# One fused decoder step on one Trainium2 core: the store of a finished output tile moves from the sync engine's queue to GpSimd's

## Chip, cores and metric

One core of one Trainium2 chip runs the whole kernel. The metric is the device time of one execution in microseconds (us). The kernel before takes 1848.58 us, the median of three runs.

## What is computed

The reference is one inference step of a hybrid decoder layer with D_MODEL 1024, for a prompt of 2048 tokens and a sample group of 8 sequences with 8 tokens each. Cut to what matters here:

```python
h = rms_norm(x, norm_pre)
proj = einsum('btd,de->bte', h, w_in)          # one projection, split below
oa = differential attention (q, k, v)           # group A
ob = causal conv + RG-LRU                       # group B
oc = rwkv7_mix(...)                             # group C: state S, token by token
od = s5_mix(...)                                # group D
o = concatenate([oa, ob, oc, od]) * silu(gate)
y = x + rms_norm(einsum('bte,ed->btd', o, w_out), norm_post)
```

The change concerns the last line only: `y` is made in 17 tiles, sixteen of 128 tokens by 1024 columns (512 KB) and one of 64 tokens for the sample group.

## The kernel before

The program runs through stages: input norm and projection, attention over the prompt, attention of the samples beside the S5 group, and at the end (from about 1170 us on) the RWKV group for the 16 prompt blocks and the samples together with the output projection. Only that last stage matters here.

An RWKV block of 128 tokens is a step of the last stage. `rw_prep` (L1105) loads its projections (`r_X`, L1114, and `r_xv`, L1117) and makes decays and keys. `rw_mats` (L1182) forms small matrices on TensorE, masks them on VectorE (L1207, L1209, L1211) and reduces their diagonal blocks to the tile `r_de` (L1214). `r_de` is stored to a small DRAM tensor `zd` (L1217) and read back, spread over groups of partitions, as `r_zr` (L1221), both by the sync engine. `rw_base` (L1252) then inverts the diagonal blocks in 15 dependent steps on VectorE, each one product into `r_x16w` (L1262) and one addition (L1263); the first product needs `r_zr`. `rw_tri`, `rw_chain` and `rw_norm` finish the block: the recurrent state `r_Z` goes through TensorE, ScalarE, GpSimd (`r_sd`, L1364) and VectorE (L1372), and the group norm gives `r_yo`.

The output of tile i goes through `out_gate` (L1514), which loads the other groups' outputs `o_o` (L1521) and the gates `o_g` (L1523, one buffer) and `o_g2` (L1525) and multiplies them on VectorE (L1526), through `out_prep` (L1532), which scales and splits the result into the float16 tile `o_h`, and through `out_tile` (L1568). `out_tile` loads the residual into `o_x` (L1573, two buffers), runs 48 matmuls (L1584), lets ScalarE take them out of PSUM into `o_y` and sum their squares (L1588, L1590), has VectorE work out the inverse norm in single-column operations (L1592 to L1594 with the helper at L99 to L111) and scale `o_y` (L1597), and has GpSimd add `o_y` into `o_x` in two halves of 512 columns (L1599; in the last tile VectorE adds the second half). L1600 stores `o_x` to `out_y`.

The order of the work is not written out by hand. The source gives an order of calls, with some matmuls tied to others; from it the framework's list scheduler, run with a timeline of its own (`schedule_with_timeline_sim=True`, L1955), makes one fixed order of instructions for each engine when the program is built. Each engine then works through its row in order, so an instruction that waits holds up all behind it. The sync engine (SP in the views) does nothing but begin transfers in this order; GpSimd is POOL, VectorE is DVE, TensorE is PE and ScalarE is ACT.

Of the kernel before, what the change touches and what calls it, by code (L numbers as in the profile page):

```python
# [53 lines left out]
class Part:  # L54
# [1513 lines left out]
    def out_tile(self, i, h, sc, pool, psum, spine=()):  # L1568

        nc = self.nc  # L1570
        t0, n = P * i, min(P, TT - P * i)
        x = pool.tile([P, D], F32, name="o_x", bufs=OB[2])
        nc.sync.dma_start(x[:n], self.i["x"][t0:t0 + n])  # L1573
        ss = pool.tile([P, 4], F32, name="o_ss", bufs=2)
        ys = []
        for g in range(2):
            sl = slice(512 * g, 512 * g + 512)
            a = psum.tile([P, 512], F32, name="acc", bufs=ACB)
            c = 0
            for k in range(KT):  # L1580
                ins = spine[(KT * g + k) * len(spine) // (2 * KT)] if spine else None
                for e, f in ((0, 0), (0, 1), (1, 0)):
                    with self.tc.issue_after(ins) if ins and e == f else ExitStack():
                        nc.tensor.matmul(a[:n].rearrange("p (c n) -> p c n", c=4), h[:, k, e], self.wo[:, 4 * g:4 * g + 4, k, f, :],  # L1584
                                         start=c == 0, stop=c == 3 * KT - 1)
                    c += 1
            y = pool.tile([P, 512], F32, name="o_y", bufs=OB[3])
            nc.scalar.activation(y[:n], a[:n], AF.Copy, scale=sc[:n, 1:2])  # L1588
            jk = pool.tile([P, 6, P], BF16, name="o_j", bufs=1)
            nc.scalar.activation(jk[:n, :4].rearrange("p a b -> p (a b)"), y[:n], AF.Square, accum_out=ss[:n, g:g + 1])  # L1590
            ys.append(y)
        nc.vector.tensor_tensor(ss[:n, 2:3], ss[:n, 0:1], ss[:n, 1:2], op=ALU.add)  # L1592
        nc.vector.tensor_scalar(ss[:n, 2:3], ss[:n, 2:3], 1.0 / D, 1e-6, op0=ALU.mult, op1=ALU.add)
        self.rsqrt(pool, ss[:n, 3:4], ss[:n, 2:3], n, 1, "oq")  # L1594
        for g, y in enumerate(ys):
            sl = slice(512 * g, 512 * g + 512)
            nc.vector.scalar_tensor_tensor(y[:n], y[:n], ss[:n, 3:4], self.npo[:n, sl], op0=ALU.mult, op1=ALU.mult)  # L1597
            eng = nc.vector if i == 15 and g else nc.gpsimd
            eng.tensor_tensor(x[:n, sl], y[:n], x[:n, sl], op=ALU.add)  # L1599
        nc.sync.dma_start(self.o["y"][t0:t0 + n], x[:n])  # L1600

    def rwkv_sample_consts(self, pool):
        nc = self.nc
# [377 lines left out]
```

## Time and profile before

| what | value |
|---|---|
| three runs | 1840.5, 1848.58, 1851.93 us |
| the profiled execution | 1846.33 us |
| span of its instructions | 1844.5 us |
| TensorE busy | 1497.3 us (81% of the span) |
| VectorE busy | 1448.1 us (79%) |
| ScalarE busy | 902.1 us (49%) |
| GpSimd busy | 811.6 us (44%) |
| granted TensorE clock, mean | 0.881 of full speed |

The span goes from the first instruction to the last; the profiled execution's own time has some two microseconds around it. The busy share of an engine is a mean over all stages and says little on one of them, so that the stage with the stores is read by itself: what each engine was busy with in it, what an engine waited for and for how long, and the order of single instructions on one engine in a stretch. In those rows the time at the front is the start in microseconds from the span's start, the next number the duration, and the bracket at the end the idle time of the engine before the instruction and what ended it. In the table by stretches the number in brackets behind a busy time is the count of instructions, and PEld is TensorE's loading of weights. In the lists of waits the three numbers are microseconds in all, times, and the longest.

### The profile page before, as it was taken

How to read it: one execution, taken by the hardware profiler on the slowest of the kernel's cores; microseconds unless marked ns; L12 is line 12 of the kernel's file. 1: busy time of each engine (PE TensorE's matmuls, PEld its weight loads, DVE VectorE, ACT ScalarE, POOL GpSimd, SP SyncE). 2: the span in 40 equal slices, each digit the busy share in tenths (PEclk: the TensorE clock that was granted, in tenths of full speed). 3: DMA queues.
4: the chain of work that ended last, by engine and by line, in shares of the span. 5: the costliest groups of instructions: out<-in, count | busy, mean ns of one | idle time of the engine just before them, and what ended most of it. 6: DMA issues, size and time to landing. Idle time of an engine off the chain costs nothing.

```text
span 1844.5 us, 33323 instructions
## 1 busy us (share of the span) xinstructions
PE 1497.3 (81%) x10956; PEld 844.9 (46%) x10956; DVE 1448.1 (79%) x4619; ACT 902.1 (49%) x2211; POOL 811.6 (44%) x887
## 2 busy tenths in 40 slices
PE   4889888987789788878894899657688887887887
PEld 2445644444344344434442456446455454554443
DVE  7797639988899899889896754376878887888865
ACT  3455746655556566657772222243344454444333
POOL 3441326736668877443344454261324333333312
PEclk9999998999899899989996999875777887887889
DMA  4422144575445655464447877635223233333221
GB/s 147 128 91 93 28 116 117 125 149 117 111 111 139 152 141 146 106 145 115 86 104 199 274 250 238 205 96 163 73 66 100 81 105 93 92 86 102 66 72 58
DMA packets 300898, 225.33 MB, mean 122 GB/s; under 512 B 192531, under 2 KB 248565, under 8 KB 300213
## 3 DMA queue, kind: packets, MB, share of 16 engines
q1 hardware_dynamic: 288388, 184.85, 37.4%
q10 hardware_dynamic: 8496, 24.76, 4.7%
q0 software_dynamic: 3840, 13.61, 2.6%
q8 instruction: 86, 1.41, 0.3%
q14 instruction: 88, 0.71, 0.1%
HBM read 130.04 MB, written 53.24 MB: 99 GB/s over the span
## 4 chain that ended last, share of the span: by engine, by line
DVE 34%; PE 21%; DMA 15%; issue 8%; POOL 4%; ACT 3%; SPq 1%; ACTq 0%; POOLq 0%; DVEq 0%
PE acc L206 7%; DMA r_zr<-zd 5%; DVE a_mx L365 4%; PE acc L1584 4%; DVE a_e L389 4%; DMA a_wt<-a_w 3%; DVE r_x L1263 2%; DVE r_x16w L1262 2%; DVE a_w L395 2%; DMA zd<-r_de 2%; PE ss L511 2%; DVE r_W L1177 1%; PE pf L530 1%; POOL a_e L388 1%; POOL a_w L395 1%
## 5 line engine op out<-in xcount | busy, mean ns | idle before, releaser
L206 PE MATMUL acc<-hT,w 128*128 128x512 f16 (+1 forms) x3120 | 633.6, 353 | 24.7 <-ACT pst L640 4.3
L206 PEld LDWEIGHTS <-w 128*128 128x128 f16 x3120 | 269.7, 101 | 322.3 <-issue 66.8
L368 ACT ACTIVATE a_e<-s,a_mx,sig 128x512 f32<-128x512 f32 (+3 forms) x320 | 226.9, 715 | 122.6 <-DVE a_mx L366 106.4
L1584 PE MATMUL acc<-wo,o_h 128*128 128x512 f16 (+1 forms) x816 | 225.1, 422 | 1.2 <-ACT o_y L1588 0.6
L365 DVE TENSOR_REDUCE a_mx<-s 128x1 f32<-128x512 f32 (+3 forms) x320 | 186.3, 599 | 23.4 <-PE s L361 18.7
L388 POOL TENSOR_SCALAR a_e<-a_e,a_al 128x512 f32<-128x512 f32 (+3 forms) x160 | 114.6, 731 | 148.6 <-DVE a_al L384 119.4
L389 DVE SCALAR_TENSOR_TENSOR a_e<-a_e,a_al 128x512 f32<-128x512 f32 (+3 forms) x160 | 149.3, 948 | 9.2 <-POOL a_e L388 9.0
L361 PE MATMUL s<-kh,qh 128*128 128x512 f16 (+3 forms) x320 | 105.7, 359 | 38.2 <-ACT a_e L368 35.0
L402 PE MATMUL pv<-vtok,a_wt 128*128 128x128 f16 x544 | 70.0, 230 | 64.6 <-DMA a_wt<-a_w 57.9
L392 ACT CAST a_w<-a_e 128x512 f16<-128x512 f32 (+3 forms) x160 | 86.3, 557 | 69.9 <-DVE a_e L389 63.5
L1584 PEld LDWEIGHTS <-o_h 128*128 128x128 f16 (+1 forms) x816 | 76.6, 105 | 95.1 <-issue 26.3
L395 POOL TENSOR_TENSOR a_w<-a_e,a_w 128x512 f16<-128x512 f32 (+3 forms) x80 | 90.0, 1128 | 64.4 <-ACT a_w L392 62.4
L1262 DVE TENSOR_TENSOR r_x16w<-r_zr,r_x 128x60 f32<-128x60 f32 (+18 forms) x255 | 58.8, 231 | 67.0 <-DMA r_zr<-zd 63.8
L1599 POOL TENSOR_TENSOR o_x<-o_y,o_x 128x512 f32<-128x512 f32 (+1 forms) x33 | 48.4, 1487 | 121.4 <-DVE o_y L1597 84.7
L402 PEld LDWEIGHTS <-a_wt 128*128 128x128 f16 x544 | 52.2, 104 | 91.4 <-DMA a_wt<-a_w 76.1
L395 DVE TENSOR_TENSOR a_w<-a_e,a_w 128x512 f16<-128x512 f32 (+2 forms) x80 | 76.9, 964 | 2.7 <-ACT a_w L392 2.7
L170 POOL TENSOR_TENSOR hT<-hf,hT 128x512 f16<-128x512 f32 (+1 forms) x36 | 36.5, 1022 | 88.3 <-ACT hT L168 88.2
L403 PE MATMUL pv<-vtok,a_wt 128*128 128x64 f16 x544 | 66.1, 202 | 0.0
L1263 DVE TENSOR_TENSOR r_x<-r_x,r_x16w 128x60 f32<-128x60 f32 (+18 forms) x255 | 62.4, 245 | 3.4
L368 ACT ACTIVATION_READ_ACCUMULATOR a_e<-s,a_mx,sig 128x1 f32 x320 | 64.0, 200 | 0.0
L366 DVE TENSOR_SCALAR a_mx<-a_mx,sig 128x1 f32<-128x1 f32 x320 | 59.8, 201 | 0.4
L511 PE MATMUL ss<-kv,qbd 128*32 128x256 f32 x256 | 52.5, 415 | 6.7 <-DMA kv<-in_ckv 6.5
(552 smaller groups left out, 3378.0 us busy)
## 6 DMA issues: line engine op xcount, KB each, us to landing
kv<-in_ckv SPq DMA_DIRECT2D x128, 256.0 KB
w<-in_w_in ACTq DMA_DIRECT2D x20, 512.0 KB
pc<-pst SPq DMA_DIRECT2D x40, 256.0 KB
xw<-in_xT SPq DMA_DIRECT2D x16, 512.0 KB
w<-in_w_out ACTq DMA_DIRECT2D x16, 512.0 KB
sg<-pst SPq DMA_DIRECT2D x32, 256.0 KB
r_X<-pc SPq DMA_DIRECT2D x16, 512.0 KB
r_zr<-zd SPq DMA_DIRECT2D x16, 512.0 KB
```

The costliest lines, as they stand in the source:

```text
L206: self.nc.tensor.matmul(acc[:, :n], w16[:, k, a, :], h[:, k, e, :], start=(c == 0), stop=(c == 3 * KT - 1))
L361: ins = nc.tensor.matmul(s[:, :kn], q[:, c], kh[:, c, k0:k0 + kn], start=True, stop=True)
L365: nc.vector.tensor_reduce(mx[:, p, c:c + 1], s[:, :kn], axis=AX.X, op=ALU.max, negate=True)
L368: nc.scalar.activation(e[:, :kn], s[:, :kn], AF.Exp, scale=sig, bias=mx[:, p, c:c + 1], accum_out=l[:, p, c:c + 1])
L388: nc.gpsimd.tensor_scalar(e1[:, :kn], e1[:, :kn], al[:, p, 1:2], 0.0, op0=ALU.mult, op1=ALU.add)
L389: nc.vector.scalar_tensor_tensor(e0[:, :kn], e0[:, :kn], al[:, p, 0:1], e1[:, :kn], op0=ALU.mult, op1=ALU.add)
L395: eng.tensor_tensor(w[:, kn:], e0[:, :kn], w[:, :kn], op=ALU.subtract)
L402: ins = nc.tensor.matmul(pv[:, :P], wt[:, j], v, start=kt == 0, stop=kt == qb, skip_group_check=True)
L511: ins = nc.tensor.matmul(sp[g:g + 32, 256 * j:min(256 * j + 256, n)], self.qbd[:, m, s].rearrange("p a q -> p (a q)"), rhs, start=True, st ...
L1262: XV.tensor_tensor(w[:, :, :m], zr[:, k, :, k + 1:], x[:, :, k:k + 1].to_broadcast([P, nu, m]), op=ALU.mult)
L1263: XV.tensor_tensor(x[:, :, k + 1:], x[:, :, k + 1:], w[:, :, :m], op=ALU.add)
L1584: nc.tensor.matmul(a[:n].rearrange("p (c n) -> p c n", c=4), h[:, k, e], self.wo[:, 4 * g:4 * g + 4, k, f, :], start=c == 0, stop=c == 3 * ...
```

## The change

The store of `o_x` to `out_y` is issued by GpSimd in place of the sync engine. Nothing else in the source differs.

```diff
             eng = nc.vector if i == 15 and g else nc.gpsimd
             eng.tensor_tensor(x[:n, sl], y[:n], x[:n, sl], op=ALU.add)
-        nc.sync.dma_start(self.o["y"][t0:t0 + n], x[:n])
+        nc.gpsimd.dma_start(self.o["y"][t0:t0 + n], x[:n])
```

The scheduler makes its orders anew from this source, and from the first store on they differ on every engine. On GpSimd, around the addition into the `o_x` of one tile in the middle of the stage, the row before is:

```order
L1599 TENSOR_TENSOR o_x_19963<-o_y_19991,o_x_19963 128x512
L1599 TENSOR_TENSOR o_x_19963<-o_y_20020,o_x_19963 128x512
L1163 TENSOR_SCALAR r_kf_20623<-r_tha_20575,rwv_15083 128x128
L1139 TENSOR_SCALAR r_thw_20576<-r_thw_20576 128x256
L1163 TENSOR_SCALAR r_kf_20623<-r_tha_20575,rwv_15083 128x128
L1165 TENSOR_SCALAR r_kka_20622<-r_tha_20575 128x256
L1167 TENSOR_TENSOR r_kf_20623<-r_kf_20623,r_X_20562 128x256
L1364 TENSOR_TENSOR r_sd_20362<-r_Z_19862,r_Dp_19752 64x128 x2
```

and now it is:

```order
L1599 TENSOR_TENSOR o_x_19963<-o_y_19991,o_x_19963 128x512
L1599 TENSOR_TENSOR o_x_19963<-o_y_20020,o_x_19963 128x512
L1139 TENSOR_SCALAR r_thw_20576<-r_thw_20576 128x256
L1163 TENSOR_SCALAR r_kf_20623<-r_tha_20575,rwv_15083 128x128
L1165 TENSOR_SCALAR r_kka_20622<-r_tha_20575 128x256
L1600 DMA out_y<-o_x_19963 128x1024
L1167 TENSOR_TENSOR r_kf_20623<-r_kf_20623,r_X_20562 128x256
L1364 TENSOR_TENSOR r_sd_20362<-r_Z_19862,r_Dp_19752 64x128 x2
```

The store stands behind L1139, L1163 and L1165 and not directly behind the addition that it needs. Of the first eleven stores eight stand behind L1165 in this way and three behind the first L1163. The sync engine's row at the same tile is, before:

```order
L1221 DMA r_zr_20254<-zd1_15089 128x1x1024
L1117 DMA r_xv_20977<-pc_1197 128x2x64 x2
L1525 DMA o_g2_20951<-sg3_1201 128x2x128
L1600 DMA out_y<-o_x_19963 128x1024
L1573 DMA o_x_20789<-in_x 128x1024
L1521 DMA o_o_21360<-od3_63 128x6x128
L1114 DMA r_X_21388<-pc_1197 128x8x128
```

and now:

```order
L1221 DMA r_zr_20254<-zd1_15089 128x1x1024
L1525 DMA o_g2_20951<-sg3_1201 128x2x128
L1573 DMA o_x_20789<-in_x 128x1024
L1521 DMA o_o_21360<-od3_63 128x6x128
L1114 DMA r_X_21388<-pc_1197 128x8x128
```

The store has gone, while the load of `o_x_20789` into the same buffer, which has to wait for that store to land, stands where it stood. (The two loads of `r_xv` are now ahead of L1221.) On VectorE the rows that lead up to the same step's `r_de` are, before:

```order
L1209 TENSOR_TENSOR r_ET_20232<-ra_20233,rmask_15067 64x256
L110 SCALAR_TENSOR_TENSOR oq1_20026<-oq1_20026,o_ss_19965 128x1
L1207 TENSOR_TENSOR r_W_20221<-ra_20241,rmask_15067 64x512
L1209 TENSOR_TENSOR r_ET_20232<-ra_20241,rmask_15067 64x256
L1211 TENSOR_TENSOR r_dg_20249<-r_NA_20231,bm4_15077 128x256
L111 SCALAR_TENSOR_TENSOR r_nrs_20092<-nq4_20101,r_nrs_20092 128x4
L111 SCALAR_TENSOR_TENSOR o_ss_19965<-oq1_20026,o_ss_19965 128x1
L1214 TENSOR_REDUCE r_de_20251<-r_dg_20249 128x64
```

and now:

```order
L1593 TENSOR_SCALAR o_ss_19965<-o_ss_19965 128x1
L1207 TENSOR_TENSOR r_W_20221<-ra_20241,rmask_15067 64x512
L1209 TENSOR_TENSOR r_ET_20232<-ra_20241,rmask_15067 64x256
L1211 TENSOR_TENSOR r_dg_20249<-r_NA_20231,bm4_15077 128x256
L1421 TENSOR_SCALAR r_nss_20091<-r_nss_20091 128x4
L99 TENSOR_SCALAR o_ss_19965<-o_ss_19965 128x1
L1526 TENSOR_TENSOR o_o_20947<-o_o_20947,o_g_20949 128x768
L1214 TENSOR_REDUCE r_de_20251<-r_dg_20249 128x64
```

The product L1526, whose end frees the buffer of `o_g` for its next load, now stands right ahead of `r_de`, and the single-column rows of the norm (`o_ss`, `oq`) come later. L1526 stands between `r_dg` and `r_de` in four of the eleven steps from the first store on before, and in six now. Between `r_de` and the first product with `r_zr` VectorE has 247 rows over these eleven steps before and 293 now; the 46 more are nearly all small rows of the two norms.

## Rows read from the trace of the kernel before

**Rows 1.** Two stretches: length, busy PE, PEld, DVE, ACT, POOL, clock, DMA share, GB/s.

```profile
1411.50:1752.00 340.50, 284.03 (x2504) 165.16 (x2503) 285.21 (x1108) 146.80 (x412) 123.89 (x170) 0.82 0.32 90
1752.00:1844.50 92.50, 72.98 (x526) 35.42 (x522) 54.67 (x228) 34.84 (x89) 19.24 (x18) 0.91 0.20 65
```

**Rows 2.** Who VectorE waited for, 1411.5 to 1752: us in total, times, longest.

```profile
DVE r_x16w L1262 <- DMA r_zr<-zd: 39.7, 10, 6.6
...
DVE o_o L1526 <- DMA o_o<-od: 1.4, 2, 1.0
```

**Rows 3.** Who the sync engine's queue waited for, 1380 to 1845.

```profile
SPq L1600 <- POOL o_x L1599: 74.5, 11, 12.1
```

**Rows 4.** The sync engine's transfers in order of time, at two tiles.

```profile
1416.86 0.35 SPq L1600 DMA_DIRECT2D out_y<-o_x  x1
1423.93 0.36 SPq L1525 DMA_DIRECT2D o_g<-sg  x1
...
1663.84 0.36 SPq L1525 DMA_DIRECT2D o_g<-sg  x1
1664.29 0.42 SPq L1600 DMA_DIRECT2D out_y<-o_x  x1
1667.34 0.35 SPq L1573 DMA_DIRECT2D o_x<-in_x  x1
1673.73 0.37 SPq L1521 DMA_DIRECT2D o_o<-od  x1
```

**Rows 5.** GpSimd in order of time, at the second of these tiles.

```profile
1656.09 3.12 POOL L1599 TENSOR_TENSOR o_x<-o_y,o_x 128x512 f32<-128x512 f32 x2 [3.81 <-DVE o_y L1597]
...
1664.89 0.41 POOL L1139 TENSOR_SCALAR r_thw<-r_thw 128x256 f32<-128x256 f32 x1 [5.24 <-ACT r_thw L1137]
...
1665.83 0.51 POOL L1165 TENSOR_SCALAR r_kka<-r_tha 128x256 f32<-128x256 f32 x1
```

**Rows 6.** GpSimd's groups by line: stores that it begins elsewhere; us in all, mean ns.

```profile
L275 POOL DMA_DIRECT2D out_v<-vf x4 | 2.3, 564 | 3.2 <-ACT vtok L273 3.2
```

**Rows 7.** Transfers by issue: stores begun by GpSimd, KB each, median us to landing.

```profile
yd<-s5ys POOLq DMA_DIRECT2D x4, 528.0 KB, 5.3
...
od<-lx POOLq DMA_DIRECT2D x2, 256.0 KB, 2.6
```

**Rows 8.** The slowest of these, the loads of s5E (514 KB): us from issue to landing.

```profile
DMA to landing us min/median/max: 4.2/7.7/12.3
```

**Rows 9.** Who waited for GpSimd, 1380 to 1845: first and last of four entries.

```profile
PEld ra L49 <- POOL r_XY L1270: 1.6, 2, 0.8
...
PEld rl L44 <- POOL r_M L1283: 0.2, 1, 0.2
```

**Rows 10.** VectorE in order of time: r_de and the first product with r_zr.

```profile
1514.36 0.58 DVE L1214 TENSOR_REDUCE r_de<-r_dg 128x64 f32<-128x256 f32 x1
1524.00 0.22 DVE L1262 TENSOR_TENSOR r_x16w<-r_zr,r_x 128x60 f32<-128x60 f32 x1 [2.49 <-DMA r_zr<-zd]
1544.77 0.57 DVE L1214 TENSOR_REDUCE r_de<-r_dg 128x64 f32<-128x256 f32 x1
1555.97 0.22 DVE L1262 TENSOR_TENSOR r_x16w<-r_zr,r_x 128x60 f32<-128x60 f32 x1 [6.28 <-DMA r_zr<-zd]
1593.30 0.39 DVE L1262 TENSOR_TENSOR r_x16w<-r_zr,r_x 128x60 f32<-128x60 f32 x1 [2.63 <-DMA r_zr<-zd]
```

**Rows 11.** The sync engine at the second of these steps.

```profile
1544.88 0.36 SPq L1523 DMA_DIRECT2D o_g<-sg  x1
1545.37 0.45 SPq L1217 DMA_DIRECT2D zd<-r_de  x1
```

**Rows 12.** VectorE's groups by line, 1411.5 to 1752: a single-column row of the norm.

```profile
L110 DVE SCALAR_TENSOR_TENSOR oq<-oq,o_ss 128x1 f32<-128x1 f32 x28 | 4.3, 153 | 0.0
```

**Rows 13.** The sync engine's last transfer, from 1838 on.

```profile
1840.11 0.34 SPq L1600 DMA_DIRECT2D out_y<-o_x  x1
```

**Rows 14.** What the sync engine's queue waited for from 1840 on.

```profile
SPq L1955 <- DMA out_y<-o_x: 2.1, 1, 2.1
```

## The prediction

> **What bounds the kernel now.** I read the views in this order: busy time by stretches, VectorE's waits, the sync engine's waits, then single transfers and instructions in order of time. The stores lie in the last stage, so I begin with the stretch of ten steps from 1411.5 to 1752 us [rows 1]. VectorE is busy for 285.2 of its 340.5 us (84%) and TensorE for 284.0; GpSimd is busy for 123.9 (36%). Nobody there is idle for long, but VectorE's 55.3 us of idleness have one main cause: 39.7 us are waits for `r_zr` in front of the first product of the inversion, about 4 us a step [rows 2]. A step is therefore VectorE's work plus that wait, 34.05 us on average (340.5 over ten). The wait starts a fixed journey after `r_de` (store to `zd`, load back): in one step 9.64 us pass from the start of `r_de` to the first product and VectorE stands still for 2.49 of them, in the next 11.20 us pass and it stands still for 6.28 [rows 10]. How long it stands still depends on how many other instructions the schedule has put between `r_de` and that product, and on how long the journey takes.
>
> The sync engine looks worse than it is. It waits 74.5 us in eleven places for GpSimd's addition before it can store [rows 3], and all its later loads stand behind. But what is behind is not ready either. At 1416.86 it has its store out, and the next transfer, the load of `o_g2`, starts only at 1423.93, because it waits for VectorE [rows 4]. At the tile of 1664 the order is the other way round: the sync engine comes to the store late, at 1664.29, since `o_g2` before it waited; GpSimd had ended its addition at 1659.21 [rows 4, 5]. The view shows the wait that ended last before each transfer, not time that the kernel would get back.
>
> **The change, part by part.**
>
> The sync engine loses 17 issues of some 0.35 us and 74.5 us of waiting. What it gets for them is small, since the load of `o_x` into the stored buffer stays in its row, at about the same place, and it now has to wait there until GpSimd's store has landed. The block moves by one instruction, from the store to the reload. In the tile of 1664 the reload goes out at 1667.34 and the next transfer, `o_o`, at 1673.73 [rows 4], released by something else; `o_o` came late for VectorE by only 1.4 us in ten steps [rows 2]. I value this part at 0; the bound on the good side is those 1.4 us.
>
> GpSimd gets 17 issues. The trace has no store of 512 KB begun by it, but four of 128 KB, which occupy it for 0.564 us each [rows 6]: 17 x 0.564 = 9.6 us on an engine that is idle for 216 us in these ten steps. Behind the store stand products for the keys (L1167), the state's decay (L1364) and L1180; other engines waited for GpSimd only four times from 1380 on, 1.6 us at most and 0.2 at least in one entry [rows 9]. Cover is there, so I take +1 us; if it were gone, eleven stores in the steps would cost 11 x 0.564 = +6.2. The lower bound is 0.
>
> In eight of eleven tiles the store also comes later than GpSimd could give it, because the schedule puts it behind L1139, which waits for ScalarE. In the tile of 1664 L1165 ends at 1666.34 [rows 5], 2.05 us after the sync engine's store began. How long it then takes to land is bounded by a store of 256 KB in 2.6 us and one of 528 KB, of more scattered shape, in 5.3 [rows 7]; I take the middle, 4.0, because the size is that of the second and the shape that of the first. Then the reload goes at about 1670.4, still 3.3 us before `o_o`. Cost 0.
>
> Here the Trainium skill has a price of its own, on the page DMA: Bandwidth & Descriptors, section Anatomy of one DMA: a transfer begun by GpSimd takes about 2.0 us plus its bytes at 436 GB/s, an estimate of 3.2 us for 512 KB. The store of 256 KB took the 2.6 that this rule gives, the one of 528 KB took 2.1 us more than it. By the rule the last store, below, would cost 0.8 and not 1.6.
>
> The new order is the largest term, and it comes from the scheduler, not from the store. Between `r_de` and the first product VectorE now has 46 more rows over eleven steps, nearly all single-column rows of 0.153 us [rows 12], so 46 x 0.153 = 7.0 us of work slips into the wait for `r_zr`: -7.0. Against it, in two more steps L1526 stands right before `r_de`, which lets the load of `o_g` out just before the store to `zd`, as at 1544.88 and 1545.37 [rows 11]. That step's journey was 11.20 us against 9.64, so 2 x 1.56 = +3.1. Together -3.9. The bounds are wide, since ten steps could all become like the shortest, or the six with L1526 before `r_de` all like the long one: from first product to first product one step took 31.97 us and the next 37.33 [rows 10]. Ten short ones would give 10 x (34.05 - 31.97) = -20.8; six long ones among ten, each 37.33 - 34.05 = 3.28 over the mean, +19.7. I take the value from the row counts.
>
> At the end, the last store is on the path. The sync engine began it at 1840.11, was busy for 0.34 us and waited 2.1 more for it [rows 13, 14], so 2.4 in all. GpSimd's would take 4.0: +1.6. The bounds are 2.6 and 12.3 us [rows 7, 8], +0.2 to +9.9.
>
> Sum: 0 + 1 - 3.9 + 1.6 = -1.3 us. Against the profiled execution's own 1846.33 (its span of 1844.5 and 1.8 around it) that is 1845.0. The median of the runs is 2.25 us above that execution, so I forecast 1847.3 for a median, the old 1848.58 less 1.3. A measurement of this kernel can tell about 1% from no change, 18 us.
>
> **Rivals.**
>
> The new order is simply better: every step becomes like the one of 31.97 us. Then 1848.6 - 20.8 + 2.6 (GpSimd and the end) = 1830.4. For it speaks that VectorE's waits for `r_zr` of 39.7 us are there to be filled; against it, that the number of steps with the two long products L1597 between `r_de` and the first product is eight of eleven in both orders, so that only small rows were moved.
>
> The new order is worse at `r_de`: all six steps that have L1526 before it become long, and the moved rows do not fill their waits. That is 1848.6 + 19.7 + 2.6 = 1870.9. For it speaks the pair of steps in [rows 10]; against it, that four steps of before have L1526 there and not all are long, and that the step after a long one is shorter. It decides where zd's store is slowed by `o_g`.
>
> The store lands late: the reload then holds up `o_o` and `r_X` in the sync engine's row, and VectorE waits at L1526. The turning point is a landing time of 1673.73 - 0.35 - 1666.34 = 7.0 us. GpSimd's loads of 514 KB took 7.7 in the median and 12.3 at most [rows 8]. At 10 us the delay is 3.0 in each of eight tiles, 24 us, and 7.6 at the end, with +1: 1848.6 + 32.6 = 1881.2. Against it speaks that those loads were eight, issued in groups, while these are single stores a step apart. The Trainium skill has a reason for it, on the page DMA: Bandwidth & Descriptors, section SWDGE vs HWDGE vs iDMA: GpSimd writes the descriptors into SBUF, which VectorE can lock it out of in some of its modes, and a transfer begun by the sync engine is immune. In this trace GpSimd's issues took 0.564 us beside a working VectorE [rows 6], so nothing shows the lock yet.
>
> The change does not do what it says, in that the sync engine stays blocked at the reload, is no rival but the first term of the sum.
>
> **How the numbers follow.** Forecast 0.60, better order 0.14, worse order at `r_de` 0.17, late landing 0.09. The forecast's own range is 1837 to 1859, from the bounds of GpSimd's term, the end, and about half of the order's. Faster by over 1% (below 1830) takes most of the first rival: 0.13. Slower by over 1% (above 1867) takes nearly all of the late landing and half of the worse order, since not all six need be long: 0.18. Within 1%: 0.69. The range to hold the time 8 times in 10 goes from 1830 to 1868; it leaves out most of the late landing and the lower half of the better order.
>
> **What would show it.** Right: the sync engine's waits at L1600 are gone and its waits at L1573 for the store have grown to a similar sum; GpSimd's L1600 rows are near 0.56 us; VectorE's wait for `r_zr` over the same steps falls to about 36 us; the last store takes 4 us. Wrong: `o_o` or `r_X` turns up among VectorE's or TensorE's waits with more than a few microseconds (late landing), the wait for `r_zr` rises above 50 us (worse order), or the steps shorten by 2 us each (better order). GpSimd's stores well above 0.6 us, or other engines that wait for GpSimd for more than 10 us in all, would break the second term.

## The result and the profile after

The changed kernel takes 1858.32 us in the median (18 runs, 1851.71 to 1865.82) against 1849.63 for the one before (18 runs): a ratio of 1.0052 with a 95% interval of 1.0033 to 1.0071, so 9.6 us slower (6.1 to 13.1; the two medians by themselves lie 8.7 apart). The profiled execution took 1853.88 us with a span of 1852.1, 7.6 over the span before. That is within 1% and inside the 1837 to 1859 that were named, a range wide enough for either sign, but on the other side of the -1.3 us that were forecast.

The two stretches of [rows 1], after (columns as there):

```profile
1411.50:1752.00 340.50, 281.13 (x2479) 166.01 (x2481) 283.16 (x1103) 146.14 (x409) 127.99 (x180) 0.82 0.31 90
1752.00:1852.10 100.10, 77.51 (x545) 38.37 (x545) 57.91 (x231) 35.60 (x91) 23.36 (x25) 0.87 0.18 60
```

In the same 340.5 us VectorE got through 1103 rows where it had 1108, and 100.1 us were left to do where there had been 92.5. Who VectorE waited for from 1411.5 to 1752 (us, times, longest), against [rows 2]:

```profile
DVE r_x16w L1262 <- DMA r_zr<-zd: 33.5, 10, 7.2
DVE o_o L1526 <- DMA o_o<-od: 5.8, 2, 4.1
DVE r_W L1207 <- ACT r_NA L1206: 2.3, 2, 1.7
DVE r_ss L1152 <- PE ra L44: 2.2, 2, 1.3
DVE r_kk L1162 <- PE ra L116: 2.2, 1, 2.2
```

The wait for `r_zr` fell by 6.2 us, from 39.7. The wait for `o_o` grew by 4.4, and waits at `r_W` and `r_kk` stand where the list of before had almost none. The sync engine's largest waits from 1380 on, against [rows 3]:

```profile
SPq L1573 <- DMA out_y<-o_x: 59.4, 8, 14.6
SPq L1525 <- DVE r_x16w L1262: 39.8, 4, 14.4
```

L1600 is gone from them, and the reload L1573 waits in its place. GpSimd's stores, and below them their time to landing; [rows 6 to 8] had only other transfers:

```profile
L1600 POOL DMA_DIRECT2D out_y<-o_x x17: 567/605/622, 1386.3 to 1845.4; - x17
...
DMA to landing us min/median/max: 2.9/2.9/4.9
```

The tile that [rows 4, 5] show at 1664 us, on GpSimd and then on the sync engine:

```profile
1657.79 3.20 POOL L1599 TENSOR_TENSOR o_x<-o_y,o_x 128x512 f32<-128x512 f32 x2 [0.75 <-DVE o_y L1597]
...
1662.00 0.41 POOL L1165 TENSOR_SCALAR r_kka<-r_tha 128x256 f32<-128x256 f32 x1
1662.35 0.60 POOL L1600 DMA_DIRECT2D out_y<-o_x  x1
```

```profile
1668.71 0.41 SPq L1573 DMA_DIRECT2D o_x<-in_x  x1
1675.91 0.36 SPq L1521 DMA_DIRECT2D o_o<-od  x1
```

The store begins 1.36 us after its addition ended, and lands some 3 us later, still before the reload at 1668.71; `o_o` follows 7 us behind that.

For the rest I cut both traces at the same rows: from the first product with `r_zr` of one step to that of the step eleven later, from there to the start of VectorE's last L1562 (the last `o_h`), and from there to the end. Before, then after:

```profile
1385.70:1761.40 375.70, 312.40 (x2776) 181.09 (x2776) 313.85 (x1225) 162.01 (x452) 132.41 (x184) 0.83 0.31 90
1761.40:1821.30 59.90, 55.82 (x399) 27.39 (x399) 41.24 (x180) 25.98 (x67) 14.61 (x15) 0.91 0.18 60
1821.30:1844.50 23.20, 11.22 (x51) 4.70 (x49) 9.70 (x32) 4.22 (x9) 4.63 (x4) 0.85 0.25 79
```

```profile
1384.70:1763.30 378.60, 315.35 (x2795) 184.63 (x2796) 315.01 (x1238) 163.76 (x455) 137.80 (x195) 0.83 0.31 89
1763.30:1826.10 62.80, 55.96 (x380) 28.05 (x379) 42.19 (x167) 25.28 (x65) 16.44 (x18) 0.88 0.17 58
1826.10:1852.10 26.00, 11.24 (x51) 4.72 (x49) 9.75 (x32) 4.24 (x9) 6.51 (x7) 0.82 0.21 71
```

So 2.9 us more in the steps, 2.9 behind the last step with 19 matmuls fewer, and 2.8 at the end, less 1.0 that this execution was ahead at the start. The first two can be the new order or the stores; the experiments take the two apart.

### The profile page after: what moved, and what is told of

Read it like the earlier page. It is cut to its first block, busy times and chain, and to the rows that moved or that the text cites. A ratio compares the mean times of both kernels' runs of the same rounds, so it can differ in the third digit from the quotient of the medians.

```text
span 1852.1 us, 33295 instructions
## 1 busy us (share of the span) xinstructions
PE 1495.8 (81%) x10956; PEld 846.9 (46%) x10956; DVE 1451.7 (78%) x4619; ACT 904.2 (49%) x2211; POOL 822.0 (44%) x904
## 4 chain that ended last, share of the span: by engine, by line
DVE 32%; PE 22%; DMA 15%; issue 8%; POOL 5%; ACT 4%; SPq 1%; ACTq 0%; POOLq 0%; DVEq 0%
PE acc L206 6%; PE acc L1584 5%; DMA r_zr<-zd 5%; DVE a_mx L365 4%; DVE a_e L389 3%; DMA a_wt<-a_w 3%; DVE a_w L395 2%; DVE r_x16w L1262 2%; DMA zd<-r_de 2%; PE ss L511 1%; DVE r_x L1263 1%; POOL a_e L388 1%; PE rc L44 1%; PE pf L530 1%; DVE r_W L1177 1%
## 5 line engine op out<-in xcount | busy, mean ns | idle before, releaser
L395 POOL TENSOR_TENSOR a_w<-a_e,a_w 128x512 f16<-128x512 f32 (+3 forms) x80 | 89.7, 1124 | 59.4 <-ACT a_w L392 57.3
L1262 DVE TENSOR_TENSOR r_x16w<-r_zr,r_x 128x60 f32<-128x60 f32 (+18 forms) x255 | 66.5, 261 | 61.5 <-DMA r_zr<-zd 58.5
L1599 POOL TENSOR_TENSOR o_x<-o_y,o_x 128x512 f32<-128x512 f32 (+1 forms) x33 | 49.1, 1502 | 117.7 <-DVE o_y L1597 90.7
L1263 DVE TENSOR_TENSOR r_x<-r_x,r_x16w 128x60 f32<-128x60 f32 (+18 forms) x255 | 59.8, 235 | 3.2
L1364 POOL TENSOR_TENSOR r_sd<-r_Z,r_Dp 64x128 f32<-64x128 f32 x64 | 29.6, 463 | 72.3 <-DVE r_Z L1372 65.6
L366 DVE TENSOR_SCALAR a_mx<-a_mx,sig 128x1 f32<-128x1 f32 x320 | 60.2, 203 | 0.4
```

What stands on the lines that cost most here:

```text
L395: eng.tensor_tensor(w[:, kn:], e0[:, :kn], w[:, :kn], op=ALU.subtract)
L1262: XV.tensor_tensor(w[:, :, :m], zr[:, k, :, k + 1:], x[:, :, k:k + 1].to_broadcast([P, nu, m]), op=ALU.mult)
L1263: XV.tensor_tensor(x[:, :, k + 1:], x[:, :, k + 1:], w[:, :, :m], op=ALU.add)
```

## The experiments

**How the order is held.** Both programs trace the same instructions under the same numbers; only the engine of 17 of them differs. So a kernel can be given any wanted row: a table lists, for each engine from just before the first store on, the numbers in order, and each is tied behind the one ahead of it, without a wait.

```diff
         program(tc, ins, outs)
+        pin(tc)
...
+def pin(tc):
+    rows = {i.name: i for i in tc.nc.cur_bb.bb.instructions}
+    dep = mybir.DependencyInfo(mybir.DependencyClass.NoSync, mybir.DependencyReason.DATA)
+    for row in ROWS.split(";"):
+        n, last = 0, None
+        for d in row.split():
+            n += int(d)
+            i = rows[f"I-{n}"]
+            if last:
+                tc.add_manual_dep(i, last, dep, reason="row")
+            last = i.name
```

The old order is that of before, the new one that of after. The table itself costs nothing that can be seen: old_sync_quarters, which is before with its stores in quarters, has a ratio of 1.0003, and new_pool_direct, which is after with its stores a few rows earlier, 1.0050 where after has 1.0052. All runs in one table; the times in us are from one trace each, cut as above, "last step" being the eleventh step and "close" the time from the end of VectorE's last L1599 to the end of the span (good to some 0.05 us, since spans are read in tenths). The ratio is that of times to the kernel before, with its interval.

| run | order, stores | 11 steps | last step | behind it | close | ratio |
|---|---|---|---|---|---|---|
| before | old, sync | 375.7 | 29.3 | 59.8 | 4.45 | |
| after | new, GpSimd | 378.7 | 33.2 | 62.8 | 7.22 | 1.0052 (1.0033 to 1.0071) |
| old_order_pool | old, GpSimd | 376.0 | 30.4 | 59.5 | 7.24 | 1.0033 (1.0004 to 1.0061) |
| new_order_sp | new, sync | 376.2 | 33.4 | 62.9 | 4.46 | 1.0030 (1.0003 to 1.0056) |
| old_order_last_pool | old, last GpSimd | 373.4 | 30.3 | 57.9 | 6.34 | 1.0026 (1.0001 to 1.0052) |
| new_order_last_sp | new, last sync | 381.3 | 33.8 | 61.6 | 5.52 | 1.0080 (1.0047 to 1.0113) |
| new_last_sp_again | the same | 379.4 | 33.8 | 62.0 | 5.49 | 1.0044 (1.0022 to 1.0067) |
| new_then_old | mixed, sync | 373.2 | 30.3 | 57.9 | 4.14 | 1.0011 (0.9989 to 1.0033) |
| old_then_new | mixed, sync | 377.4 | 32.0 | 61.4 | 4.44 | 1.0028 (1.0002 to 1.0053) |
| new_yc_early | new, sync | 376.6 | 34.2 | 60.2 | 4.45 | 1.0004 (0.9983 to 1.0024) |
| after_yc_early | new, GpSimd | 375.1 | 33.6 | 60.2 | 7.25 | 1.0053 (1.0034 to 1.0073) |
| new_pool_direct | new, GpSimd | 379.6 | 33.6 | 62.6 | 7.30 | 1.0050 (1.0028 to 1.0071) |
| new_og_late | new, sync | 374.7 | 34.5 | 61.9 | 4.14 | 1.0045 (1.0023 to 1.0067) |
| old_fill | old, sync | 366.4 | 31.2 | 58.1 | 4.22 | 0.9962 (0.9940 to 0.9984) |
| old_fill2 | old, sync | 368.5 | 30.5 | 55.3 | 4.17 | 0.9941 (0.9918 to 0.9964) |
| old_pool_but_last | old, last sync | 370.6 | 30.2 | 59.3 | 5.51 | 1.0006 (0.9987 to 1.0025) |
| old_pool_quarters | old, last sync | 378.9 | 30.9 | 60.3 | 9.17 | 1.0040 (1.0022 to 1.0058) |
| old_sync_quarters | old, sync | 375.3 | 30.7 | 60.2 | 4.19 | 1.0003 (0.9986 to 1.0019) |

An interval is some 4 us to either side, so a term of 3 us is not read from one run's time. The columns of single stretches repeat far better: the last step took 29.3 to 30.9 us in the six traces with nothing but the old order and 33.2 to 33.8 in the five with nothing but the new one, the stretch behind it 57.9 to 60.3 and 61.6 to 62.9.

**Order and store apart.** old_order_pool:

```diff
  L1599 TENSOR_TENSOR o_x<-o_y,o_x 128x512 x2
+ L1600 DMA out_y<-o_x
  L1163 TENSOR_SCALAR r_kf<-r_tha,rwv 128x128
```

> The order of every engine is held as in the kernel before, by a table of instruction numbers; only the 17 stores move, each from the sync engine's row to GpSimd's, directly behind the addition that it needs. The changed kernel was 9.6 us over the one before. Theory O (the new order costs it, the store itself only at the end of the program): 2.5 to 3 us over before, all of it behind the last addition. Theory S (the store on GpSimd's row and its later landing cost it): 7 to 10 us over before, with o_o among VectorE's waits as in the changed kernel (5.8 us) and GpSimd's later rows awaited. Theory Q (neither, a change of the whole program such as code or semaphores): under 1 us.

new_order_sp (the same source lines as before; on the sync engine's row):

```diff
  L1525 DMA o_g2<-sg3
+ L1600 DMA out_y<-o_x
  L1573 DMA o_x<-in_x
```

> The order of every engine is held as in the changed kernel; only the 17 stores move back to the sync engine's row, ahead of the load into the same buffer, as they stood before. Theory O: 6 to 7 us over before (the 9.6 less the end's 2.8), with steps of the last stage 0.3 us longer on average than in before and the same stretch behind the last step longer by 2 to 3 us. Theory S: within 2 us of before. Under O, VectorE's waits for r_zr over the steps stay near the changed kernel's 41.6 us; under S the longer steps go.

Each of the two alone costs something: 6.1 us for the store in the old order (0.7 to 11.3) and 5.5 for the order (0.6 to 10.3). In the traces the store adds nothing to the steps of the old order and 2.8 us to the close; the order adds to the last step and the stretch behind, with the stores back on the sync engine and the waits for `o_o` unchanged at 5.7 us. In old_order_pool they are 1.0 us over the same steps. So that wait belongs to the order. By the times alone neither theory can be ruled out, since both intervals reach into what theory S expected; it is the columns and these waits that speak for theory O.

**The end.** old_order_last_pool and new_order_last_sp:

```diff
-        nc.sync.dma_start(self.o["y"][t0:t0 + n], x[:n])
+        (nc.gpsimd if i == 15 else nc.sync).dma_start(self.o["y"][t0:t0 + n], x[:n])
```

```diff
-        nc.gpsimd.dma_start(self.o["y"][t0:t0 + n], x[:n])
+        (nc.sync if i == 15 else nc.gpsimd).dma_start(self.o["y"][t0:t0 + n], x[:n])
```

> Order held as in the kernel before, and only the store of the last tile goes to GpSimd's row, at its end. Theory E (the last store is the whole cost of the store's engine): 2.5 to 3 us over before, the time from the end of VectorE's last addition to the end of the span growing from 4.5 to about 7.2 us. If the landing of a store begun by GpSimd is not slower and only its issue is (0.59 against 0.34): under 1 us.

> Order held as in the changed kernel with its stores on GpSimd, but the store of the last tile goes back to the sync engine. Theory O with E: 2.5 to 3 us under the changed kernel, so 6 to 7 over before. If E is wrong and the end is not what the last store makes it: as the changed kernel, 9 to 10 over before. Theory S allows either, and differs from O by the run with the new order and all stores on the sync engine, which would then be 4 us or more below this one.

Theory E in its simple form falls. The close is 6.34 us with the last store alone on GpSimd, not 7.2, and 5.52 with all but the last there, not 4.45: the sixteen stores that had landed long before add to it as well. The time of new_order_last_sp was above that of the changed kernel and not 3 us under it; the repeat gave 8.1 us over before, so the pair lies around 11 with intervals that overlap. The 8.1 (4.1 to 12.4) lies between what theories A and B expected of the repeat and does not tell them apart.

**Where the order costs.** new_then_old follows the new order up to the first product of the last but one prompt step and then the old, old_then_new the other way round.

> All stores on the sync engine. The rows follow the new order up to the first product of the last but one prompt step and the old order from there. Over three traces of each order the ten steps up to there differ by -6.9 to +6.3 us each and by +0.3 in sum; the last step is 3.5 us longer in the new order and the stretch behind it 3.3. Theory T (the loss of the new order sits in the last step and the stretch behind it): within 1.5 us of before. Theory D (the loss is spread, the prefix leaves work undone that the rest must do): 3 us or more over before, with the last step and the stretch behind it longer than the old order's 30.0 and 59.1 us.

> All stores on the sync engine. The rows follow the old order up to the same place and the new order from there. Theory T: 6 to 7 us over before, the last step near 33.5 us and the stretch from its first product to the last o_h near 62.4. Theory D: 0 to 3 us over before.

Theory T holds by the columns: with ten steps of the new order and the old rest the last step and the stretch behind it are as short as in the old order (30.3 and 57.9), and the time is 1.0011; with the old steps and the new rest the stretch behind is long (61.4) and the time is 1.0028, 5.2 us over before (0.4 to 9.8). Its last step took 32.0, half way and not the 33.5 expected, and both intervals of the time also hold what theory D expected. Single steps differ far more than their sum: the fifth took 38.4 us in the new order and 32.1 in the old, the sixth 30.4 and 37.3 (means of three traces).

In the last step the front of `r_de` is later because more stands ahead of it. From the first product to the end of `r_de`, before and after:

```profile
1732.10:1752.60 20.50, 17.99 (x159) 10.79 (x161) 18.98 (x75) 7.01 (x16) 6.79 (x10) 0.84 0.23 62
```

```profile
1730.10:1754.00 23.90, 22.06 (x204) 13.01 (x204) 21.13 (x78) 9.63 (x27) 7.21 (x12) 0.78 0.25 77
```

The stretch is 3.4 us longer and holds 45 matmuls more, with 4.1 us more of TensorE's time: it is busy for 22.06 of 23.90. That these 45 are the cause is read from the rows, and was not tried by itself. For the stretch behind, VectorE, GpSimd and TensorE in the changed kernel:

```profile
1763.34 0.22 DVE L1262 TENSOR_TENSOR r_x16w<-r_zr,r_x 128x60 f32<-128x60 f32 x1 [5.29 <-DMA r_zr<-zd]
1763.48 0.16 DVE L110 SCALAR_TENSOR_TENSOR nq<-nq,r_nss 128x4 f32<-128x4 f32 x1
1763.55 1.41 DVE L1597 SCALAR_TENSOR_TENSOR o_y<-o_y,o_ss,npo 128x512 f32<-128x512 f32 x2
...
1765.01 1.25 DVE L111 SCALAR_TENSOR_TENSOR r_nrs<-nq,r_nrs 128x4 f32<-128x4 f32 x1
...
1766.31 1.48 DVE L1423 TENSOR_TENSOR r_yc<-r_yc,r_nrs 128x256 f32<-128x256 f32 x1
```

```profile
1764.38 3.13 POOL L1599 TENSOR_TENSOR o_x<-o_y,o_x 128x512 f32<-128x512 f32 x2 [11.97 <-DVE o_y L1597]
```

```profile
1767.93 0.66 PE L49 MATMUL rl<-ident,r_yc 128*128 128x128 f32 x2 [3.05 <-DVE r_x L1263]
...
1770.60 5.36 PE L1584 MATMUL acc<-wo,o_h 128*128 128x512 f16 x15
```

and TensorE before:

```profile
1763.98 0.66 PE L49 MATMUL rl<-ident,r_yc 128*128 128x128 f32 x2 [5.05 <-DVE o_ss L111]
...
1771.11 3.40 PE L1584 MATMUL acc<-wo,o_h 128*128 128x512 f16 x15
```

TensorE needs `r_yc` for L49. Before it has it 2.6 us after the first product (1763.98, the cut at 1761.40), in the changed kernel 4.6, because the two long products L1597 and what they push back stand ahead of L1423. L1597 also lets GpSimd's addition L1599 begin, and beside it L111 takes 1.25 us and L1423 1.48 (elsewhere the same two rows take 0.18 and 0.41, as at 1385.91 and 1386.34 before); the rows do not say why. VectorE stood still for 5.29 us just before, with the two rows and L1423 nearly ready. And 15 matmuls of the same form then take 5.36 us and not 3.40: the granted clock from 1770.6 to 1776.0 was 0.63 in the mean, and from 1767.9 to 1771.0 it was 0.50, which is the lower of the two levels (1.2 GHz); ahead of that, to 1767.9, TensorE had done nothing for 3.0 us. Before, the idleness was longer (5.05 us) but lay earlier, and for these 15 the clock was back (1.00 from 1771.1 to 1774.6). new_yc_early and after_yc_early move three rows:

```diff
+ L110 SCALAR_TENSOR_TENSOR nq<-nq,r_nss 128x4
+ L111 SCALAR_TENSOR_TENSOR r_nrs<-nq,r_nrs 128x4
+ L1423 TENSOR_TENSOR r_yc<-r_yc,r_nrs 128x256
  L1262 TENSOR_TENSOR r_x16w<-r_zr,r_x 128x60
- L110 SCALAR_TENSOR_TENSOR nq<-nq,r_nss 128x4
  L1597 SCALAR_TENSOR_TENSOR o_y<-o_y,o_ss,npo 128x512 x2
  L1263 TENSOR_TENSOR r_x<-r_x,r_x16w 128x60
- L111 SCALAR_TENSOR_TENSOR r_nrs<-nq,r_nrs 128x4
  L1262 TENSOR_TENSOR r_x16w<-r_zr,r_x 128x56
- L1423 TENSOR_TENSOR r_yc<-r_yc,r_nrs 128x256
```

> New order, stores on the sync engine, and only in the last prompt step three rows of VectorE (L110 and L111 of the group norm, and L1423, which makes r_yc) go from behind the first product of the inversion and two products L1597 to directly ahead of it, into the wait for r_zr. Theory M (the stretch behind the last step is longer because TensorE stands still for r_yc and then works at the lower clock): the stretch falls from 62.4 us to 59 or 60, TensorE's wait of 3.2 us for VectorE at L49 goes, and the time is 2 to 3 us over before in place of 5. Theory N (it is longer for other rows of the new order): the stretch stays at 61.5 to 63 us.

> The changed kernel with the same three rows moved, stores on GpSimd. Theory M: 6 to 7 us over before in place of 9.6, the stretch behind the last step 59 to 60 us. Theory N: 9 to 10 over before, the stretch 61.5 to 63.

TensorE in new_yc_early, whose first product stands at 1759.11:

```profile
1759.48 0.63 PE L49 MATMUL rl<-ident,r_yc 128*128 128x128 f32 x2
1763.57 0.48 PE L44 MATMUL rc<-r_Z,r_W 128*64 128x64 f32 x2 [3.45 <-DVE r_Z L1372]
...
1765.64 4.02 PE L1584 MATMUL acc<-wo,o_h 128*128 128x512 f16 x15
```

Theory M holds for the stretch, 60.2 us in both kernels in place of 62.4. Not all as expected: L49 now follows at once, but the idleness moves to the next link, the state `r_Z`: beside L1599 it is now rows of the inversion ahead of it that take 1.28 us (L1263) and 1.18 (L1262). From the first product to the end of the 15 matmuls it is 10.6 us in place of 12.6; 0.7 of the 2.1 come from the earlier start of the 15 and 1.3 from their shorter time (5.36 against 4.02). The time shows it with the stores on the sync engine (1.0004 in place of 1.0030) and not with them on GpSimd (1.0053, 9.8 us over before), where theory N's 9 to 10 us came.

**What moving rows on VectorE is worth.** new_og_late moves one row in eight places. In six of them it stood directly ahead of `r_de`, as below; in the other two it stood six and nine rows ahead:

```diff
- L1526 TENSOR_TENSOR o_o<-o_o,o_g 128x768
  L1214 TENSOR_REDUCE r_de<-r_dg 128x64
+ L1526 TENSOR_TENSOR o_o<-o_o,o_g 128x768
```

> New order, stores on the sync engine, and one row moved on VectorE: where L1526 stands just ahead of r_de (eight places, six of them in the measured steps) it goes directly behind it, so that r_de no longer waits for L1526 and for the load of o_o in front of it. Theory W (VectorE's row is the path: what leaves the front of r_de and falls into the wait for r_zr is gained): the o_o waits of 5.7 us and six times 0.96 us go, 11 us together, so 4 to 5 us under before. Theory G (what is gained at one wait comes back at another): o_o's waits go from the list, but the time falls by 4 us or less, to 2 us or more over before.

No gain: 8.3 us over before. The largest wait stayed, since its L1526 stands ten rows ahead of `r_de` and was not among the eight; VectorE's wait for `o_o` in the steps of this kernel:

```profile
DVE o_o L1526 <- DMA o_o<-od: 4.1, 1, 4.1
```

So what that wait of 4.1 us costs was not tried. Of the eight L1526 that went behind `r_de` no cost can be seen: the steps (374.7 us against 376.2) changed by less than they scatter, and the time did not fall.

old_fill and old_fill2, in the old order, move L1526 in its four places in the same way and bring rows of the norms, in two steps together with L1597, ahead of the first product; one of the places:

```diff
+ L111 SCALAR_TENSOR_TENSOR r_nrs<-nq,r_nrs 128x4
+ L1423 TENSOR_TENSOR r_yc<-r_yc,r_nrs 128x256
  L1262 TENSOR_TENSOR r_x16w<-r_zr,r_x 128x60
- L111 SCALAR_TENSOR_TENSOR r_nrs<-nq,r_nrs 128x4
...
- L1423 TENSOR_TENSOR r_yc<-r_yc,r_nrs 128x256
```

> Old order, stores on the sync engine, only VectorE's row changed: L1526 goes behind r_de in its four steps (0.96 us each), and rows of the two norms that are ready go from behind the first product of the inversion to ahead of it, into the wait for r_zr, in four steps (worked out 0.5, 2.2, 2.2 and 3.7 us). Nothing else moves. Theory W: 3.8 + 8.6 = 12 us under before. Theory G: r_zr's waits fall by as much, from 47.9 us, but the time by less than half of it.

> As the run with rows filled into the wait in the old order, with more of them: in eight further steps six to eleven small rows of the norm of the keys (0.75 to 1.38 us a step, 9.4 us together) go ahead of the first product. Theory W (a row moved into the wait is gained): 7.6 us of the first run and 9 more, 16 to 17 us under before. Theory G (these steps have another limit, or the rows were hidden where they stood): 6 to 10 us under before.

VectorE's wait for `r_zr` from 1380 on, in old_fill and then in old_fill2 (47.9 us in twelve places before):

```profile
DVE r_x16w L1262 <- DMA r_zr<-zd: 35.9, 12, 5.6
```

```profile
DVE r_x16w L1262 <- DMA r_zr<-zd: 17.4, 12, 3.2
```

and the eleven steps of both by stretches:

```profile
1388.80:1755.20 366.40, 311.48 (x2800) 181.02 (x2801) 313.98 (x1242) 163.41 (x457) 134.66 (x187) 0.85 0.32 92
```

```profile
1392.80:1761.30 368.50, 316.83 (x2797) 183.00 (x2794) 328.32 (x1242) 163.23 (x456) 134.17 (x186) 0.83 0.32 92
```

old_fill is 7.0 us faster than before (3.0 to 11.1) and so beats both kernels; the two steps out of which L1597 and L1423 had gone went from 37.5 to 32.7 and from 37.3 to 33.9 us. Of the 12.0 us that left the wait 7.0 came back in the time, more than the half that theory G allowed and less than the 12 of theory W; the interval reaches into the first and ends short of the second. old_fill2 takes another 18.5 us out of the wait and gets nothing for it in the steps (its time, 10.9 us under before, overlaps with old_fill's): VectorE is busy for 328.3 us with the same 1242 rows, 14.3 more. Theory G holds for the small rows. Their place in the row of before shows why. A product and its addition of 56 columns with two small rows between them (before), and the same two without (old_fill2):

```profile
1761.97 0.21 DVE L1262 TENSOR_TENSOR r_x16w<-r_zr,r_x 128x56 f32<-128x56 f32 x1
1762.10 0.15 DVE L110 SCALAR_TENSOR_TENSOR nq<-nq,r_nss 128x4 f32<-128x4 f32 x1
1762.17 0.15 DVE L109 TENSOR_TENSOR oq<-o_ss 128x1 f32<-128x1 f32 x1
1762.24 0.21 DVE L1263 TENSOR_TENSOR r_x<-r_x,r_x16w 128x56 f32<-128x56 f32 x1
```

```profile
1761.78 0.22 DVE L1262 TENSOR_TENSOR r_x16w<-r_zr,r_x 128x56 f32<-128x56 f32 x1
1762.03 0.22 DVE L1263 TENSOR_TENSOR r_x<-r_x,r_x16w 128x56 f32<-128x56 f32 x1
```

From the start of the product to that of its addition it is 0.27 us with two small rows between and 0.25 with none: the addition needs the product, and what stands between starts while the product still runs. So a small row there costs some 0.01 us, not its 0.15.

**Stores on GpSimd: place and number.** new_pool_direct puts each store behind its addition:

```diff
  L1599 TENSOR_TENSOR o_x<-o_y,o_x 128x512 x2
+ L1600 DMA out_y<-o_x
  L1139 TENSOR_SCALAR r_thw<-r_thw 128x256
  L1163 TENSOR_SCALAR r_kf<-r_tha,rwv 128x128
  L1165 TENSOR_SCALAR r_kka<-r_tha 128x256
- L1600 DMA out_y<-o_x
```

> The changed kernel's order with the stores on GpSimd, each directly behind the addition that it needs in place of behind L1163 or L1165. Theory L (the late store holds up the load of o_x and what stands behind it on the sync engine): 2 us or more under the changed kernel, that is 7.5 us or less over before. Theory K (the place of the store in GpSimd's row costs nothing, only that it ends the program does): 8 to 11 us over before.

Theory K: 9.2 us over before, as the changed kernel. No cost of the store's lateness can be seen. old_pool_but_last has the source line of new_order_last_sp in the old order; the two with quarters cut fifteen stores:

```diff
-        nc.sync.dma_start(self.o["y"][t0:t0 + n], x[:n])
+        for q in range(4 if i < 15 else 1):
+            m = 32 if i < 15 else n
+            (nc.sync if i == 15 else nc.gpsimd).dma_start(self.o["y"][t0 + m * q:t0 + m * q + m], x[m * q:m * q + m])
```

> Old order; sixteen stores on GpSimd, each directly behind its addition, the last on the sync engine. Theory A (a store on GpSimd costs only where it ends the program): 0 to 1 us over before. Theory B (each store also costs some 0.2 to 0.3 us in the steps): 3 to 5 us over before, with the eleven steps at 377 us or more against 375.

> As the run with sixteen stores on GpSimd in the old order, but fifteen of them are cut into four of 32 rows each, so GpSimd begins 45 transfers more. At 0.59 us each they occupy it 26.6 us longer. Theory A: as that run, within 2 us. Theory B with a cost per issue: 9 us or more over that run, with other engines waiting for GpSimd.

> Old order, all stores on the sync engine, the same fifteen cut into four. Shows what the cut itself costs: both theories expect before, within 2 us, since 45 issues of 0.35 us on the sync engine lie in waits.

> The run with the changed kernel's order and stores, the last one on the sync engine, a second time. Theory A: 6 to 7 us over before (5.5 for the order, 1 for the end). Theory B: 9 to 10. The first time it was 13 in the median; a second 13 would mean that both lack a term.

In the old order sixteen stores on GpSimd cost 1.1 us (theory A), and 45 issues more did not make other engines wait for GpSimd: the largest such waits are 1.5 and 1.2 us with the quarters on GpSimd, 1.4 and 1.2 with them on the sync engine. old_pool_quarters is 7.4 us over before (4.1 to 10.7), 6.3 over old_pool_but_last: theory A allowed 2 there and theory B wanted 9, so neither gave the size. Of the 7.4, 4.7 are its close of 9.17, which neither foresaw. Its steps, 378.9, are the longest of the six traces of the old order, 2.9 over the next; whether the 45 issues cost that is not shown. On the sync engine no cost of the quarters can be seen (0.6 us, -2.6 to 3.5). The three ends, the last addition and the last store, in old_order_last_pool, old_pool_but_last and old_pool_quarters, whose spans end at 1843.0, 1843.9 and 1857.9:

```profile
1835.03 1.63 DVE L1599 TENSOR_TENSOR o_x<-o_y,o_x 128x512 f32<-128x512 f32 x1
1837.27 0.61 POOL L1600 DMA_DIRECT2D out_y<-o_x  x1 [1.15 <-DVE o_x L1599]
```

```profile
1836.72 1.67 DVE L1599 TENSOR_TENSOR o_x<-o_y,o_x 128x512 f32<-128x512 f32 x1
1838.45 0.34 SPq L1600 DMA_DIRECT2D out_y<-o_x  x1
```

```profile
1847.10 1.63 DVE L1599 TENSOR_TENSOR o_x<-o_y,o_x 128x512 f32<-128x512 f32 x1
1848.80 0.34 SPq L1602 DMA_DIRECT2D out_y<-o_x  x1
```

## Why the prediction was wrong, point by point

**The sync engine, 0: right.** The block moved from the store to the reload (74.5 us at L1600, 59.4 at L1573), and new_pool_direct, with the stores earlier, was no faster (9.2 us over before).

**GpSimd, +1 with a bound of +6.2: right in the old order.** The issues took 0.605 us where 0.564 was used (the four stores of 528 KB at L1019, nearer in size, had occupied GpSimd for 0.603 before), and cost 1.1 us in old_pool_but_last, all of which the close accounts for (5.51 against 4.45). In the new order it is less clear: five traces with the stores on GpSimd have 378.8 us for the steps and three on the sync engine 375.8, longer in nine of the eleven steps, and after_yc_early did not get back what new_yc_early did. Whether the stores cost up to 3 us there stays open.

**The landing: too long, without effect.** I took 4.0 us; it is 2.9 in the median. The Trainium skill's rule (DMA: Bandwidth & Descriptors, Anatomy of one DMA) gave an estimate of 3.2 and was nearer. The late landing as a rival fell: `o_o` waits equally with the stores on the sync engine.

**The new order, -3.9: the step that failed.** It measured 5.5 us of loss (0.6 to 10.3) with the stores on the sync engine. It went wrong in two ways. First the price: 46 small rows at 0.153 us were counted as 7.0 us of gain. The wait for `r_zr` did fall, by 6.2 us over the ten steps where 3.9 had been worked out, so the sign that I had named came true; but rows that leave the inversion save only the 0.01 us or so that they cost there. Ten steps came out 0.7 us longer (345.4 against 344.7, the means of five and six traces). Four of these five have stores on GpSimd; the three traces of the new order and its variants with the stores on the sync engine have 341.8, inside the 340.4 to 348.0 of the old order, so that a small gain in the ten steps is not ruled out. Second the place: the sum stopped at the steps, and the loss is in the last step (33.6 against 30.3) and the stretch behind it (62.4 against 59.5), which no term of mine covered: in the last step 45 matmuls more stand ahead of `r_de` (read from the rows, not tried), and behind it `r_yc` comes after two long products (new_yc_early took back 2.2 of the 2.9). These are 3.3 + 2.9 = 6.2 us of traces. The rival of a worse order had the right sign and the wrong mechanism: L1526 ahead of `r_de` is not what costs (new_og_late).

**The end, +1.6: mis-sized, 2.8.** The store went out 0.5 us later and its data moved until about 3.1 us after the addition in place of 2.1; that is the 1.0 which landing explains. The rest comes after the data, in the close that grows with the number of transfers on GpSimd.

Together 0.7 + 6.2 + 2.8 = 9.7 us from the traces, against 9.6 measured. That they meet so closely is luck, since the time has an interval of 3.5 us to either side and the ten steps scatter by as much. That the time stayed within 1% came about because no term was large, not because the sum was right.

## What to carry to other kernels

Where a scheduler makes the order, one moved instruction is two changes: hold the order by a table and try the instruction and the order apart before explaining either. A wait in an engine's list is not a price: filling it pays only with rows that cost their full time where they stood, so look at start-to-start times there, and at who waits for the row that is pushed back. Sum the last step and the way to the end by themselves; steps in the middle make up for each other, the last one has nobody behind it.

## What the runs showed of the hardware that I had not expected

The close of the program grows with the number of transfers begun by GpSimd: 4.14 to 4.46 us with all stores on the sync engine, 5.5 with sixteen of them on GpSimd and 9.17 with 61, the last store being on the sync engine each time (the 45 further transfers on the sync engine in old_sync_quarters leave it at 4.19), so (9.17 - 5.5) / 45 = 0.08 us a transfer, and 6.34 and 7.2 with one and seventeen when the last is GpSimd's. The trace has no row that says what is done there.

In the changed kernel and in the one before the last transfer's bytes move alike. The rows give GB/s in each fortieth of 1838 to 1845 (before) and of 1843 to 1853 (after):

```profile
GB/s 0 0 0 0 0 0 0 0 0 0 0 0 0 0 0 0 117 421 398 421 445 398 398 398 0 0 0 0 0 0 0 0 0 0 0 0 47 0 0 0
```

```profile
GB/s 0 0 0 0 0 0 0 0 0 0 0 0 0 0 246 475 442 393 426 115 0 0 0 0 0 0 0 0 0 0 0 0 0 0 0 0 0 0 0 0
```

The store's bytes end at 1842.2 and at 1848.0 us (the lone 47 is of another queue), and the spans 2.3 and 4.1 us later.

Of the lock that the Trainium skill describes (DMA: Bandwidth & Descriptors, SWDGE vs HWDGE vs iDMA), which would hold up GpSimd's descriptors beside some modes of VectorE, no run shows a sign in the issues: the seventeen took 567 to 622 ns beside a VectorE that was busy for 83% of the ten steps, and quarters of a store 489 to 579 ns. Why the longest landing was 4.9 us and the median 2.9 is not shown.
